# A hybrid decoder step: six first products ahead of 1/rms, the last two FFN groups by token halves, finished blocks parked tile by tile

## Chip, core and metric

The kernel runs on one core of a Trainium2 chip. The metric is the device time of one execution in microseconds; the median of three executions of the kernel before is 3283.72 us (3283.42 to 3285.11). A core has a matrix engine (TensorE, PE in the rows), a vector engine (VectorE, DVE), a scalar engine (ScalarE, ACT), GpSimd (POOL) and a queue that only issues transfers (SyncE, SP). Each engine takes its instructions in order; between engines there are semaphores. TensorE multiplies out of SBUF into PSUM banks, and the other engines read the banks. TensorE's clock is granted by a throttle; the windows show it as a share of full speed, and 0.50 and 1.00 are its two levels (1.2 and 2.4 GHz).

## What is computed

One layer for 2048 prompt tokens and 64 new tokens (8 sequences of 8), with a final norm. Shortened:

```python
h = rmsnorm(x, norm_attn); p = h @ w_in
o_attn = attention(q, k, v); o_rwkv = rwkv7_mixer(...)
gates = sigmoid(p[..., e4:] + b_gate)
merged = gates[..., :D] * (o_attn @ w_branch_attn) + gates[..., D:] * (o_rwkv @ w_branch_rwkv)
x = x + merged @ w_out
u = rmsnorm(x, norm_ffn) @ w_ffn_in; gp, vp = u[..., :D_FF], u[..., D_FF:]
c = cb + sum(cw[j] * buf[:, j:j + T] for j in range(3))      # buf: gp with two rows of state ahead
x = x + (gelu(c) * vp) @ w_ffn_out
y = rmsnorm(x, norm_final)                                    # x * rsqrt(mean(x*x) + 1e-6) * g
```

The outputs are y, the attention windows, and the shift, wkv and convolution states of both kinds of sequences. D is 1024, D_FF is 2816 (22 tiles of 128).

## The kernel before

The 2112 tokens go through the layer in three blocks b of T = 704 tokens. Activations lie with channels on the 128 partitions, so x of a block is 8 tiles of 128 x 704, and a block's tokens are worked on in two halves of 384 and 320 (`HALF`). A product is `mm3`: both operands are split into a high and a low part, and each step of 128 in depth takes three matmuls, 24 for a depth of 1024, 12 and 6 for the FFN's output products over 4 or 2 tiles of D_FF. A weight tile comes through `unit`: SP loads 512 KB into a raw buffer (L339, two of them), ScalarE casts the high part (L340), VectorE subtracts for the low part (L341), into one of two `wp` buffers. Products take PSUM banks of the pool `psd` (three), other work those of `psr` (three) and `psc` (two).

`start` begins the first block. It loads x by halves, scales and squares it, and multiplies the weight tiles js = (18, 19) with the unnormalised x, since 1/rms is a factor per token that can come later: three of four products go into the three `psd` banks, the fourth waits until one is free. 1/rms of a half is `rowsums` (L416 on TensorE), a chain of eleven small instructions on VectorE (`rms`, `rsqrt`, L423, L375 to L380), a transposition on TensorE (`turned`, L1039) and a copy to `rb0` on ScalarE (L488); `timed` (L508) is the multiplication that empties a bank. `proj` takes the products made ahead from `ahead`.

Each block then goes through projections, attention and the recurrent mixer, `branches` (L1346 to L1362: two half-depth products per half, gates on VectorE, the result into the tile `ms`, named `o` in the rows), `merge` and `ffn`. `ffn` takes the 22 tiles f in the groups GRP of 4, 4, 4, 4, 4 and 2: first products and activation for each f into the tile `ff` (L1432 to L1448), then the output products that are added to x (L1459 to L1461), 16 per group. In a group of 4 the halves alternate, in the last group of 2 the first half goes ahead of the second. After the last addition to a tile of x, `done` squares it (L394 on ScalarE, L395 on VectorE).

In blocks 0 and 1 the finished x is parked in DRAM: `final` issues one transfer per half on ScalarE's queue, after the half's last tile (L1477). The next block's `ms` tile of `branches` lies on the memory of that x, and so waits for the transfer. The final norm of a parked block is done later in a side stream (`final_steps`), which a planner puts between the products by a clock of estimated costs.

In block 2 `final_last` norms in place after all products: both halves' row sums, chains and transpositions, the copies to `rbl` (L1518), then for odd k a scale on ScalarE (L1521) and a product on GpSimd (L1522), for even k one instruction on VectorE (L1529), and eight transfers of tile pairs to the output yT on SP (L1530).

## Time and profile before

| | us |
|---|---|
| median of three executions | 3283.72 (3283.42 to 3285.11) |
| the profiled execution, its own time | 3283.15 |
| its span in the trace | 3281.2 |
| TensorE busy in it | 3242.3 |
| idle of TensorE ended by the first weight | 7.6 |
| idle ended by 1/rms and its use at the start | 4.7 and 2.5 |
| idle ended by `branches`' gate products, once | 3.8 |
| from TensorE's last big product to the end of the span | 18.3 |

TensorE is busy for 99% of the span, at a mean granted clock of 0.992. The last row runs from 3262.9 (the products that begin at 3247.22 last 15.64 us) to 3281.2. An engine's idle time is written at the instruction that ended it, with the instruction that released it.

### The profile page before, as it was taken

How to read it: one execution, taken by the hardware profiler on the slowest of the kernel's cores; microseconds unless marked ns; L12 is line 12 of the kernel's file. 1: busy time of each engine (PE TensorE's matmuls, PEld its weight loads, DVE VectorE, ACT ScalarE, POOL GpSimd, SP SyncE). 2: the span in 40 equal slices, each digit the busy share in tenths (PEclk: the TensorE clock that was granted, in tenths of full speed). 3: DMA queues.
4: the chain of work that ended last, by engine and by line, in shares of the span. 5: the costliest groups of instructions: out<-in, count | busy, mean ns of one | idle time of the engine just before them, and what ended most of it. 6: DMA issues, size and time to landing. Idle time of an engine off the chain costs nothing.

```text
span 3281.2 us, 60116 instructions
## 1 busy us (share of the span) xinstructions
PE 3242.3 (99%) x24072; PEld 3128.9 (95%) x24072; DVE 2029.4 (62%) x4596; ACT 1219.5 (37%) x2278; POOL 39.8 (1%) x104
## 2 busy tenths in 40 slices
PE   8999999999999999999999999999999999999998
PEld 7999999999999988899999999999999999999998
DVE  6676667745555576666555678755456575555555
ACT  4455433343323566623222323332223233222323
POOL 0000000000000000000000000000000000000000
PEclk9999999999999999999999999999999999999999
DMA  4644454545555633222433363253313272222222
GB/s 133 192 140 126 133 161 140 149 143 155 179 176 186 196 104 105 88 69 83 140 121 121 123 222 105 79 173 112 111 63 130 84 238 93 65 71 66 70 71 70
DMA packets 335016, 408.78 MB, mean 125 GB/s; under 512 B 110480, under 2 KB 261008, under 8 KB 334480
## 3 DMA queue, kind: packets, MB, share of 16 engines
q1 hardware_dynamic: 330576, 399.17, 39.0%
q10 hardware_dynamic: 4160, 5.77, 0.5%
q8 instruction: 189, 3.10, 0.4%
q14 instruction: 91, 0.75, 0.1%
HBM read 307.41 MB, written 98.41 MB: 124 GB/s over the span
## 4 chain that ended last, share of the span: by engine, by line
PE 96%; DVE 1%; ACT 1%; DMA 1%; issue 0%; POOL 0%; SPq 0%; POOLq 0%; DVEq 0%; ACTq 0%
PE psd L354 83%; PE psr L978 2%; PE psr L681 1%; PE psr L729 1%; PE psr L716 1%; PE psc L1148 1%; PE psc L1178 1%; PE psc L1181 1%; PE psr L868 1%; DMA xd<-x 0%; PE psc L1005 0%; PE psr L966 0%; PE psc L1183 0%; PE psc L1175 0%; PE psr L1005 0%; PE psc L1277 0%
## 5 line engine op out<-in xcount | busy, mean ns | idle before, releaser
L354 PE MATMUL psd<-o,wp 128*128 128x320 f32 (+1 forms) x8640 | 1443.7, 325 | 4.1 <-DVE m L1356 3.8
L354 PEld LDWEIGHTS psd<-o,wp 128*128 128x128 f32 x8640 | 1392.6, 188 | 16.3 <-issue 8.0
L354 PE MATMUL psd<-h,wp 128*128 128x320 f32 (+1 forms) x5184 | 911.7, 329 | 12.3 <-ACT wp L340 7.6
L354 PEld LDWEIGHTS psd<-h,wp 128*128 128x128 f32 x5184 | 838.1, 189 | 25.4 <-ACT wp L340 7.6
L340 ACT CAST wp<-wr 128x1024 fp32r<-128x1024 f32 x354 | 371.1, 1048 | 669.1 <-PE psd L354 643.3
L354 PE MATMUL psd<-ff,wp 128*128 128x384 f32 (+1 forms) x3168 | 536.1, 327 | 0.0
L341 DVE TENSOR_TENSOR wp<-wr,wp 128x1024 fp32r<-128x1024 f32 x354 | 432.8, 1222 | 164.9 <-ACT wp L340 157.8
L354 PEld LDWEIGHTS psd<-ff,wp 128*128 128x128 f32 x3168 | 515.3, 189 | 4.2 <-issue 1.0
L1461 DVE TENSOR_TENSOR x<-x,psd 128x384 f32<-128x384 f32 (+1 forms) x288 | 148.2, 519 | 200.7 <-PE psd L354 199.5
L1432 DVE TENSOR_TENSOR gb<-psd,rb 128x64 f32<-128x64 f32 (+2 forms) x154 | 70.5, 470 | 197.7 <-PE psd L354 195.2
L1433 ACT ACTIVATE cc<-gb,pt 128x64 f32<-128x64 f32 (+2 forms) x154 | 95.5, 636 | 209.4 <-DVE gb L1432 207.5
L1435 DVE SCALAR_TENSOR_TENSOR cc<-gb,pt,cc 128x704 f32<-128x704 f32 (+1 forms) x132 | 121.9, 924 | 2.2 <-ACT cc L1433 1.7
L1425 DVE TENSOR_TENSOR up<-psd,rb 128x384 f32<-128x384 f32 (+1 forms) x132 | 68.8, 521 | 64.4 <-PE psd L354 64.1
L1444 ACT ACTIVATE cc<-cc 128x704 f32<-128x704 f32 x66 | 52.4, 794 | 140.0 <-DVE cc L1435 82.9
L346 DVE TENSOR_TENSOR ff<-cc,ff 128x384 fp32r<-128x384 f32 (+1 forms) x132 | 68.5, 520 | 32.2 <-ACT ff L345 32.1
L1295 ACT ACTIVATE g<-psd,der 128x384 f32<-128x384 f32 (+1 forms) x64 | 35.5, 554 | 140.4 <-PE psd L354 89.2
L345 ACT CAST ff<-cc 128x384 fp32r<-128x384 f32 (+1 forms) x132 | 64.0, 486 | 61.6 <-DVE cc L1447 61.4
L624 ACT ACTIVATE s<-s,nm 128x256 f32<-128x256 f32 (+2 forms) x136 | 65.8, 486 | 39.0 <-DVE nm L619 36.8
L1447 DVE TENSOR_TENSOR cc<-cc,up 128x384 f32<-128x384 f32 (+1 forms) x132 | 68.9, 523 | 18.0 <-ACT cc L1444 14.5
L1356 DVE SCALAR_TENSOR_TENSOR m<-gt,psd 128x384 f32<-128x384 f32 (+1 forms) x96 | 49.6, 518 | 36.3 <-PE psd L354 35.5
L823 ACT ACTIVATE xs<-psd,der 128x384 f32<-128x384 f32 (+1 forms) x56 | 31.1, 555 | 107.4 <-PE psd L354 107.4
L395 DVE TENSOR_TENSOR acc<-acc,sq 128x384 f32<-128x384 f32 (+1 forms) x126 | 65.2, 518 | 6.2 <-ACT sq L394 5.5
(255 smaller groups left out, 2782.3 us busy)
## 6 DMA issues: line engine op xcount, KB each, us to landing
wr<-in_w_fi SPq DMA_DIRECT2D x132, 512.0 KB, 3.5
wr<-in_w_in SPq DMA_DIRECT2D x108, 512.0 KB, 3.7
wr<-in_w_fo SPq DMA_DIRECT2D x66, 512.0 KB, 3.5
cm<-md SPq DMA_DIRECT2D x33, 512.0 KB, 5.1
gt<-gd SPq DMA_DIRECT2D x48, 352.0 KB, 4.3
md<-m SPq DMA_DIRECT2D x48, 256.0 KB, 2.7
wr<-in_w_br SPq DMA_DIRECT2D x24, 512.0 KB, 4.3
wr<-in_w_out SPq DMA_DIRECT2D x24, 512.0 KB, 3.9
```

The costliest lines, as they stand in the source:

```text
L340: nc.scalar.copy(w[:, 0], raw)
L341: nc.vector.tensor_tensor(w[:, 1], raw, w[:, 0].bitcast(F32), op=ALU.subtract)
L346: self.nc.vector.tensor_tensor(lo, src, hi.bitcast(F32), op=ALU.subtract)
L354: nc.tensor.matmul(ps[:, :n], w[:, a, wk * 128:(wk + 1) * 128], act[:, k0 + k, b, c0:c0 + n], start=(start and k == 0 and j == 0), stop=(s ...
L624: nc.scalar.activation(s[:nq, h, :nk], s[:nq, h, :nk], ACT.Exp, bias=nm[:nq, h:h + 1], scale=0.125, accum_out=rs[:nq, h:h + 1])
L978: nc.tensor.matmul(pss[r_][:, c * 128:(c + 1) * 128], kb[rows, u + c], ar[rows, u + c], start=True, stop=True)
L1425: nc.vector.tensor_tensor(up[:, c0:c0 + n], ps[:, :n], rb[:, c0:c0 + n], op=ALU.mult)
L1432: nc.vector.tensor_tensor(dst, view(ps, 0), view(rb, c0), op=ALU.mult)
L1433: nc.scalar.activation(view(c, c0), dst, ACT.Identity, bias=self.par("cb", f), scale=cw[2])
L1435: nc.vector.scalar_tensor_tensor(c[:, :npr], gb[:, u:u + npr], cw[u], c[:, :npr], op0=ALU.mult, op1=ALU.add)
L1447: nc.vector.tensor_tensor(cv, cv, up[:, c0:c0 + n], op=ALU.mult)
L1461: nc.vector.tensor_tensor(xv, xv, ps[:, :n], op=ALU.add)
```

## The change

Three places change.

In `start` three weight tiles instead of two, (18, 19, 10), are multiplied ahead of 1/rms: six products in the three `psd` and the three `psr` banks, in the order first halves of 18 and 19, second halves of both, both halves of 10. `timed` is called for all six when `proj` takes them.

In `ffn` the loop's body is split into `first` and `second`, whose code is that of before. In the last block the groups from f = 16 (4 tiles) and from f = 20 (2 tiles) go together: the first products of all six f, then the output products of the first half for both groups, then those of the second half for both. The four weight tiles of the group from 16 are kept in `room`, on memory of the pool `old` that is free by then, the two of the other group in `wp`. The norm of the first half is a generator, stepped after six of the eight products of the group from 16 in the second half: row sums, transposition, and then VectorE's scalings with their transfers. After the last product only the second half is normed, with three of its eight tiles by ScalarE and GpSimd.

In `final` each tile of x is parked by its own transfer, 16 per block instead of two, right after the tile's square.

The diff, cut: the body of `first` is that of the loop before, indented otherwise.

```diff
@@ -460,7 +460,7 @@
-        js = (18, 19)
+        js = (18, 19, 10)
...
-        ps = [[self.dbank() for _ in js], [self.dbank()]]
+
+        banks = iter([self.bank(k) for k in "dddrrr"])
+        ps = {}
-        for u in range(2):
-            self.mm3(ps[0][u], w[u], self.h, *HALF[0])
-            if u == 0:
-                r = rms(0)
-        spread(r, 0)
-        self.mm3(ps[1][0], w[0], self.h, *HALF[1])
-        r = rms(1)
-        first = self.timed(ps[0][0], 0)
-        ps[1].append(self.dbank())
-        self.mm3(ps[1][1], w[1], self.h, *HALF[1])
-        spread(r, 1)
-        self.ahead = {js[0]: lambda: [first, self.timed(ps[1][0], 1)],
-                      js[1]: lambda: [self.timed(ps[hf][1], hf) for hf in range(2)]}
+        for u, hf in ((0, 0), (1, 0), (0, 1), (1, 1), (2, 0), (2, 1)):
+            if u == 2 and hf == 0:
+                w.append(self.unit(self.i["w_in"][js[2]]))
+            ps[u, hf] = next(banks)
+            self.mm3(ps[u, hf], w[u], self.h, *HALF[hf])
+            if u == 1:
+                r = rms(hf)
+                spread(r, hf)
+        self.ahead = {j: lambda u=u: [self.timed(ps[u, hf], hf) for hf in range(2)] for u, j in enumerate(js)}
...
-    def ffn(self, b, x, h2, rb, mp, done):
...
-        for f0, nf in GRP:
-            ft = mp.tile([P, 4, 2, T], F32R, tag="ff", name="ff")
-            for q in range(nf):
...
+        def first(f0, q, ft):
+
+            f = f0 + q
+            gb = mp.tile([P, 722], F32, tag="gb", name="gb")
...
+        def second(f0, nf, ft, order, ws, to=None, norm=None):
+
             per = 8 // nf
-            order = [(j, h) for j in range(8) for h in range(2)]
-            if per == 4:
-                order.sort(key=lambda u: u[1])
-            ws = {}
             for j, hf in order:
                 if j // per not in ws:
-                    ws[j // per] = self.unit(self.i["w_fo"][f0 + j // per])
+                    ws[j // per] = self.unit(self.i["w_fo"][f0 + j // per], None if to is None else to[:, j // per])
                 c0, n = HALF[hf]
                 ps = self.dbank()
                 self.mm3(ps, ws[j // per], ft, c0, n, nk=nf, wk0=(j % per) * nf)
@@ -1461,6 +1457,27 @@
                 nc.vector.tensor_tensor(xv, xv, ps[:, :n], op=ALU.add)
                 if f0 + nf == FF:
                     done(hf, j)
+                if norm and nf == 4 and j not in (1, 3):
+                    next(norm, None)
+
+        halves = [[(j, h) for j in range(8)] for h in range(2)]
+        for f0, nf in GRP[:-2] if last else GRP:
+            ft = mp.tile([P, 4, 2, T], F32R, tag="ff", name="ff")
+            for q in range(nf):
+                first(f0, q, ft)
+            second(f0, nf, ft, sum(halves, []) if nf == 2 else [(j, h) for j in range(8) for h in range(2)], {})
+        if last:
+
+            room = self.bigtile(dead, "o")[:].rearrange("p a b c -> p (a b c)")
+            fts = [mp.tile([P, 4, 2, T], F32R, tag="ff", name="ff"),
+                   room[:, 8192:8192 + 4 * T].rearrange("p (a b c) -> p a b c", a=2, b=2)]
+            for (f0, nf), ft in zip(GRP[-2:], fts):
+                for q in range(nf):
+                    first(f0, q, ft)
+            tos, ws = (room[:, :8192].rearrange("p (a b c) -> p a b c", a=4, b=2), None), ({}, {})
+            for order in halves:
+                for (f0, nf), ft, to, w in zip(GRP[-2:], fts, tos, ws):
+                    second(f0, nf, ft, order, w, to, norm if order[0][1] else None)
 
@@ -1473,10 +1490,9 @@
             self.square(accs[hf][:, :n], x[:, j, c0:c0 + n], j, n)
-            if j == KT - 1:
-                nc.scalar.dma_start(self.xd[b][:, :, c0:c0 + n], x[:, :, c0:c0 + n])
-                if hf:
-                    self.push("n", self.final_steps(b, accs))
+            nc.scalar.dma_start(self.xd[b][:, j, c0:c0 + n], x[:, j, c0:c0 + n])
+            if j == KT - 1 and hf:
+                self.push("n", self.final_steps(b, accs))
...
@@ -1510,33 +1526,35 @@
 
         def norm(hf):
             c0, n = HALF[hf]
-            yield 0.2
             r = self.rms(self.rowsums(accs[hf], n, "r"), "r")
-            yield 0.2
+            yield
             pb = self.turned(r, "r")
-            rb = fp.tile([P, 384], F32, tag=("cc", "up")[hf], name="rbl")
-            nc.scalar.copy(rb[:, :n], pb[:, :n])
-            for k in range(1, KT, 2):
-                xv = x[:, k, c0:c0 + n]
-                nc.scalar.activation(xv, xv, ACT.Copy, scale=self.par("norm_final", k))
-                nc.gpsimd.tensor_tensor(xv, xv, rb[:, :n], op=ALU.mult)
-                if hf == 0:
-                    yield
-            if hf == 0:
-                yield 60.0
+            if hf:
+                rb = fp.tile([P, 384], F32, tag="up", name="rbl")
+                nc.scalar.copy(rb[:, :n], pb[:, :n])
+            yield
             for k in range(0, KT, 2):
-                xv = x[:, k, c0:c0 + n]
-                nc.vector.scalar_tensor_tensor(xv, xv, self.par("norm_final", k), pb[:, :n], op0=ALU.mult, op1=ALU.mult)
+                for u in range(2):
+                    xv = x[:, k + u, c0:c0 + n]
+                    if u and hf and k < 6:
+                        nc.scalar.activation(xv, xv, ACT.Copy, scale=self.par("norm_final", k + u))
+                        nc.gpsimd.tensor_tensor(xv, xv, rb[:, :n], op=ALU.mult)
+                    else:
+                        nc.vector.scalar_tensor_tensor(xv, xv, self.par("norm_final", k + u), pb[:, :n],
+                                                       op0=ALU.mult, op1=ALU.mult)
                 nc.sync.dma_start(self.o["yT"][:, k:k + 2, b * T + c0:b * T + c0 + n], x[:, k:k + 2, c0:c0 + n])
+                yield
+        norms = [norm(0), norm(1)]
 
         def done(hf, j):
             c0, n = HALF[hf]
-            acc, xv = accs[hf][:, :n], x[:, j, c0:c0 + n]
-            self.square(acc, xv, j, n)
-            if j == KT - 1:
-                self.push("mn"[1 - hf], norm(hf))
-
-        return done
+            self.square(accs[hf][:, :n], x[:, j, c0:c0 + n], j, n)
+            if hf and j == KT - 1:
+                for _ in norms[1]:
+                    pass
+
+        return done, norms[0]
...
-    def ffn_stage(self, b, x, h2, rb):
+    def ffn_stage(self, b, x, h2, rb, dead=None):
...
-            self.ffn(b, x, h2, rb, fp, self.final_last(b, x, fp) if b == NB - 1 else self.final(b, x))
+            self.ffn(b, x, h2, rb, fp, *(self.final_last(b, x, fp) if b == NB - 1 else (self.final(b, x), None)), dead)
             if b == NB - 1:
-                self.drain("m", "n")
...
-        self.ffn_stage(2, *xs)
+        self.ffn_stage(2, *xs, old)
```

TensorE at the start, before (`psd<-h,wp` are big products, `psc<-ct,acc` row sums, `psc<-ct,nwyd` the transposition of 1/rms):

```order
L354 MATMUL psd<-h,wp 128x320 x15
L416 MATMUL psc<-ct,acc 128x1 x3
L354 MATMUL psd<-h,wp 128x320 x8
L1039 MATMUL psc<-ct,nwyd 128x128 x3
L416 MATMUL psc<-ct,acc 128x1 x3
L354 MATMUL psd<-h,wp 128x320 x24
L1039 MATMUL psc<-ct,nwyd 128x128 x3
L354 MATMUL psd<-h,wp 128x384 x24
L354 MATMUL psd<-h,wp 128x320 x24
```

and after:

```order
L354 MATMUL psd<-h,wp 128x320 x8
L354 MATMUL psr<-h,wp 128x320 x22
L354 MATMUL psr<-h,wp 128x384 x2
L354 MATMUL psr<-h,wp 128x320 x2
L354 MATMUL psr<-h,wp 128x384 x22
L354 MATMUL psr<-h,wp 128x320 x4
L1037 MATMUL psc<-ct,nwyd 128x128 x3
L416 MATMUL psc<-ct,acc 128x1 x3
L354 MATMUL psr<-h,wp 128x320 x18
L354 MATMUL psd<-h,wp 128x384 x24
L1037 MATMUL psc<-ct,nwyd 128x128 x3
L354 MATMUL psd<-h,wp 128x320 x24
```

The transposition of the first half's 1/rms stood behind 72 matmuls and stands behind 126 now; that of the second half stands behind all six products and one product of the next projection.

ScalarE at the passage from block 0 to block 1, before (`sq` and `acc` are squares, `wp<-wr` casts of weights, `xd<-x` the parking, `o<-m` the first result of `branches`):

```order
L391 ACTIVATE acc<-x_12416 128x320
L394 ACTIVATE sq<-x_12416 128x320 x2
L340 CAST wp<-wr 128x1024
L394 ACTIVATE sq<-x_12416 128x320 x3
L340 CAST wp<-wr 128x1024
L394 ACTIVATE sq<-x_12416 128x320
L1477 DMA xd_276<-x_12416 1024x1x320
L394 ACTIVATE sq<-x_12416 128x320
L340 CAST wp<-wr 128x1024
L1361 ACTIVATE o<-m 128x384
```

and after:

```order
L1493 DMA xd_276<-x_12416 128x320
L394 ACTIVATE sq<-x_12416 128x320
L1493 DMA xd_276<-x_12416 128x320
L340 CAST wp<-wr 128x1024
L394 ACTIVATE sq<-x_12416 128x320
L1493 DMA xd_276<-x_12416 128x320 x2
L394 ACTIVATE sq<-x_12416 128x320
L1493 DMA xd_276<-x_12416 128x320
L394 ACTIVATE sq<-x_12416 128x320
L1359 ACTIVATE o<-m 128x384
L340 CAST wp<-wr 128x1024
L1359 ACTIVATE o<-m 128x320
```

Parking transfers now stand between the squares; the first `o<-m`, which waits for all of them, follows the last square directly, ahead of a weight's cast that stood ahead of it.

VectorE at the end of block 2, before (`x<-x,psd` adds a product to x, `x<-x,pt,psr` scales a tile by 1/rms):

```order
L379 TENSOR_TENSOR nwtd<-nwtd,rmsm 128x3 x2
L380 SCALAR_TENSOR_TENSOR nwyd<-nwtd,nwyd 128x3 x2
L378 SCALAR_TENSOR_TENSOR nwtd<-nwyd 128x3
L379 TENSOR_TENSOR nwtd<-nwtd,rmsm 128x3
L380 SCALAR_TENSOR_TENSOR nwyd<-nwtd,nwyd 128x3
L1529 SCALAR_TENSOR_TENSOR x_28569<-x_28569,pt,psr 128x320 x4
L1529 SCALAR_TENSOR_TENSOR x_28569<-x_28569,pt,psr 128x384 x4
```

and after, in the second half's products:

```order
L1457 TENSOR_TENSOR x_28597<-x_28597,psd 128x320
L378 SCALAR_TENSOR_TENSOR nwtd<-nwyd 128x3
L379 TENSOR_TENSOR nwtd<-nwtd,rmsm 128x3
L380 SCALAR_TENSOR_TENSOR nwyd<-nwtd,nwyd 128x3
L1457 TENSOR_TENSOR x_28597<-x_28597,psd 128x320 x2
L1543 SCALAR_TENSOR_TENSOR x_28597<-x_28597,pt,psr 128x384 x8
L1457 TENSOR_TENSOR x_28597<-x_28597,psd 128x320 x5
L395 TENSOR_TENSOR acc<-acc,sq 128x320
L1457 TENSOR_TENSOR x_28597<-x_28597,psd 128x320
L395 TENSOR_TENSOR acc<-acc,sq 128x320
```

Eight scalings of the first half now stand between the sixth and the seventh addition of the second half's first eight.

## Rows read from the trace of the kernel before

**Rows 1.** TensorE's timeline at the start: start us, duration us, instructions [idle before <- releaser].
```profile
22.61 1.42 PE L354 MATMUL psd<-h,wp 128*128 128x320 f32 x8
28.73 0.90 PE L1039 MATMUL psc<-ct,nwyd 128*128 128x128 f32 x3 [4.70 <-DVE nwyd L380]
...
36.09 0.49 PE L1039 MATMUL psc<-ct,nwyd 128*128 128x128 f32 x3
39.04 24.98 PE L354 MATMUL psd<-h,wp 128*128 128x384 f32 x153 [2.47 <-DVE p L508]
```

**Rows 2.** VectorE's timeline at the start: a chain of 1/rms, products multiplied by it.
```profile
30.74 0.16 DVE L423 TENSOR_SCALAR rmsm<-psc 128x3 f32<-128x3 f32 x1
...
33.44 0.16 DVE L380 SCALAR_TENSOR_TENSOR nwyd<-nwtd,nwyd 128x3 f32<-128x3 f32 x1
...
38.51 0.95 DVE L508 TENSOR_TENSOR p<-psd,rb 128x320 f32<-128x320 f32 x2
```

**Rows 3.** ScalarE's timeline at the start, the copy of a turned 1/rms.
```profile
37.24 0.42 ACT L488 COPY rb<-psc 128x320 f32<-128x320 f32 x1
```

**Rows 4.** One-microsecond windows at the start; the granted clock stands ahead of the DMA share.
```profile
28.00:29.00 1.00, 0.28 (x2) 0.28 (x3) 0.56 (x4) 0.00 (x0) 0.00 (x0) 0.50 0.76 279
34.00:35.00 1.00, 1.00 (x7) 1.00 (x6) 0.00 (x0) 0.00 (x0) 0.00 (x0) 0.73 0.00 0
37.00:38.00 1.00, 0.00 (x0) 0.00 (x0) 0.64 (x1) 0.66 (x2) 0.00 (x0) 1.00 0.00 0
```

**Rows 5.** TensorE's timeline from block 0 to block 1.
```profile
1897.26 15.55 PE L354 MATMUL psd<-o,wp 128*128 128x384 f32 x96
1916.58 18.70 PE L354 MATMUL psd<-o,wp 128*128 128x384 f32 x99 [3.77 <-DVE m L1356]
```

**Rows 6.** The chain that ended last, there: start us, duration us, what.
```profile
1897.98 16.37 DMA xd<-x
```

**Rows 7.** DMA issues between 1885 and 1925: count, KB each, median us to landing.
```profile
wr<-in_w_br SPq DMA_DIRECT2D x4, 512.0 KB, 5.6
xd<-x ACTq DMA_DIRECT2D x1, 1536.0 KB, 6.0
...
xd<-x ACTq DMA_DIRECT2D x1, 1280.0 KB, 16.4
```

**Rows 8.** Windows of the same place, columns as in group 4.
```profile
1902.00:1914.00 12.00, 10.81 (x70) 10.55 (x68) 3.89 (x7) 1.05 (x1) 0.00 (x0) 1.00 1.05 403
1919.00:1920.00 1.00, 1.00 (x5) 1.00 (x4) 1.00 (x2) 0.47 (x1) 0.00 (x0) 0.50 0.37 93
1922.00:1923.00 1.00, 1.00 (x7) 1.00 (x6) 0.00 (x0) 0.00 (x0) 0.00 (x0) 0.95 0.77 254
```

**Rows 9.** ScalarE's timeline there: a square, the issue of a transfer.
```profile
1896.67 0.47 ACT L394 ACTIVATE sq<-x 128x320 f32<-128x320 f32 x1 [1.46 <-DVE x L1461]
...
1897.98 0.52 ACTq L1477 DMA_DIRECT2D xd<-x  x1
```

**Rows 10.** TensorE's timeline over the last 160 us.
```profile
3123.59 61.94 PE L354 MATMUL psd<-o,wp 128*128 128x384 f32 x384
...
3264.48 1.50 PE L416 MATMUL psr<-ct,acc 128*128 128x1 f32 x12 [1.61 <-DVE acc L395]
```

**Rows 11.** Groups from 3255 to the end: count | busy us, mean ns | idle.
```profile
L1461 DVE TENSOR_TENSOR x<-x,psd 128x320 f32<-128x320 f32 x8 | 3.9, 484 | 0.0
```

**Rows 12.** Timeline of the last 20 us: the scalings on VectorE and GpSimd.
```profile
3269.28 4.02 DVE L1529 SCALAR_TENSOR_TENSOR x<-x,pt,psr 128x320 f32<-128x320 f32 x8 [0.94 <-ACT rbl L1518]
3269.33 7.11 POOL L1522 TENSOR_TENSOR x<-x,rbl 128x320 f32<-128x320 f32 x8 [508.05 <-ACT rbl L1518]
```

**Rows 13.** DMA issues of the last 16 us.
```profile
out_yT<-x SPq DMA_DIRECT2D x4, 320.0 KB, 2.5
```

**Rows 14.** One window while the last outputs leave, columns as in group 4.
```profile
3272.00:3279.00 7.00, 0.00 (x0) 0.00 (x0) 1.31 (x3) 0.00 (x0) 4.44 (x5) 0.50 1.04 361
```

More of the change, by code (lines that the diff above doesn't have):

```diff
@@ L1396, in merge, with ffn @@
         return x, h2, rb
-    def ffn(self, b, x, h2, rb, mp, done):
+    def ffn(self, b, x, h2, rb, mp, done, norm, dead):
         nc = self.nc
@@ L1463, in ffn @@
                     done(hf, j)
+                if norm and nf == 4 and j not in (1, 3):
[6 more added lines that the diff above has]
+            second(f0, nf, ft, sum(halves, []) if nf == 2 else [(j, h) for j in range(8) for h in range(2)], {})
+        if last:
+            room = self.bigtile(dead, "o")[:].rearrange("p a b c -> p (a b c)")
[8 more added lines that the diff above has]
+                    second(f0, nf, ft, order, w, to, norm if order[0][1] else None)
     def final(self, b, x):
@@ L1512, in norm @@
             c0, n = HALF[hf]
[L1513 removed]
             r = self.rms(self.rowsums(accs[hf], n, "r"), "r")
[L1515 removed]
+            yield
             pb = self.turned(r, "r")
[L1517 to L1529 removed]
+            if hf:
+                rb = fp.tile([P, 384], F32, tag="up", name="rbl")
+                nc.scalar.copy(rb[:, :n], pb[:, :n])
+            yield
+            for k in range(0, KT, 2):
+                for u in range(2):
[3 more added lines that the diff above has]
+                        nc.gpsimd.tensor_tensor(xv, xv, rb[:, :n], op=ALU.mult)
+                    else:
+                        nc.vector.scalar_tensor_tensor(xv, xv, self.par("norm_final", k + u), pb[:, :n],
+                                                       op0=ALU.mult, op1=ALU.mult)
                 nc.sync.dma_start(self.o["yT"][:, k:k + 2, b * T + c0:b * T + c0 + n], x[:, k:k + 2, c0:c0 + n])
+                yield
+        norms = [norm(0), norm(1)]
         def done(hf, j):
             c0, n = HALF[hf]
[L1534 to L1539 removed]
+            self.square(accs[hf][:, :n], x[:, j, c0:c0 + n], j, n)
[3 more added lines that the diff above has]
+        return done, norms[0]
     def rwkv_prep(self, b, ep, sts, between):
```

80 lines of the change are left out of this document (38 added, 42 removed).

## Prediction

> **What bounds the kernel now.** The busy times on the page come first: TensorE works in 3242.3 of 3281.2 us at a mean granted clock of 0.992, so nothing can be won where it runs through; what counts is the 39 us in which it stands and the stretches at half clock. Next comes its list of waits, and then its timeline at each of them. At the start it stands for 4.70 us until the first 1/rms is there and for 2.47 us until a bank is emptied [rows 1]. Around the first stop the windows show the granted clock at 0.50, its lower level, and 0.73 in the window from 34 us, back at 1.00 after that; in the second, shorter stop it stays at 1.00 [rows 4]. At the passage from block 0 to block 1 it stands for 3.77 us [rows 5]; the chain of waits puts 16.37 us of parking transfer ahead of that [rows 6], and the clock is at 0.50 until shortly after 1922 [rows 8]. At the end the last row sums begin at 3264.48 [rows 10], and 16.7 us go by until the span ends at 3281.2, with no big product left.
>
> **The start.** Removed are both stops, 4.70 + 2.47 = 7.17, and the half clock. The 0.73 says that 0.54 of its window was at half clock, so from the restart at 28.73 to 34.54 TensorE ran at half speed, which cost 5.81 / 2 = 2.9. Together 10.1.
> What is late next: at 22.61 + 1.42 = 24.03 [rows 1] 72 of the 144 matmuls of the six products are done, 48 of 384 columns and 24 of 320. At full clock 384 matmuls, half of each size, take 61.94 us [rows 10]; split by columns that is 0.176 for one of 384 and 0.146 for one of 320. The 24 + 48 that are left take 4.2 + 7.0 = 11.2, row sums and one transposition in between 0.9 (a transposition is 0.49 [rows 1]), so the six are done at 36.2. The next product has a bank, since the first half's 1/rms is long there, and ends at 40.4; then the second half's transposition, 40.9. The product behind it needs a bank of `psd` that only the second half's 1/rms empties: the copy takes 0.42 [rows 3], two multiplications 0.95 [rows 2], so 42.3 and a stop of 1.4. The chain itself (30.74 to 33.60, 2.9 us [rows 2]) is no limit: its row sums stand 18 matmuls ahead of the end of the six, at some 33.5. The stop is shorter than the 2.47 at which the clock stayed up, so I add no half clock. Bounds: 0, if VectorE takes the two in the better order, and 3.8, if a weight's subtraction and two more instructions come first, with another 1.5 of half clock. Net -8.7, from -10.1 to -5.
>
> **Parking by tiles.** Removed at the first passage: the stop, 3.77, and half clock from 1916.58 to 1922.1 (0.95 in the window from 1922 leaves 0.1 of it), 5.5 / 2 = 2.75; together 6.5. At the second passage TensorE's waits show no stop, so nothing is to be had there. Before, 1280 KB were asked for at 1897.98 and were there at 1914.35, in traffic of 403 GB/s with the DMA engines' share at 1.05 [rows 6 to 8]; that is 78 GB/s for this transfer. Now all but four or five tiles of 160 KB are on their way before the next block's loads begin. At 78 GB/s a tile takes 2.05 us; from about 1896.5 that is 8 to 10 us for the last ones, 1905 to 1907. Needed is the memory at about 1908: TensorE then has work until 1897.26 + 15.55 = 1912.8 [rows 5], and the way from the release to its restart was 1914.35 to 1916.58, 2.2 us. So the stop goes, with little to spare. Behind the waiting first result of `branches` on ScalarE stands the cast of the third weight; it is due with the third pair of products, at the same 1912.8, and behind it a subtraction, so a late landing would show there as well.
> Added are 14 issues per block at 0.52 on ScalarE, beside a square of 0.47 [rows 9]: 1.0 per tile against 0.88 that TensorE takes for the six matmuls of a tile. ScalarE falls back by 8 x 0.12 = 1 us plus the casts of two weights, which reach TensorE a little late: I take 0.4 at each of two passages (0 to 2 each). Net -5.7, from -6.5 to -2.5 if the memory comes in time.
> Against it speaks a rule of the Trainium skill, "DMA: Bandwidth & Descriptors", section "Rules for kernel authors": many small transfers should be coalesced into one large one, and full bandwidth wants 1 MiB and more per transfer. By that rule the 16 tiles would get through later than the two halves, which is the first rival below. The trace is on neither side alone: 320 KB landed in 2.5 us on emptier queues [rows 13], 1536 KB in 6.0 [rows 7], so five small ones would take longer than one large one only if nothing overlapped.
>
> **The end.** After the last row sums begin, 16.7 us remain before. The chain, the turn and a copy to the first scaling take 3269.3 - 3264.48 = 4.8, with two halves' small instructions interleaved; one half alone I put at 4.4. From the first scaling to the end are 11.9, in which eight products on GpSimd take 7.11 and eight scalings on VectorE 4.02 [rows 12], and 2.88 MB leave. Now three on GpSimd (2.7) and five on VectorE (2.5) are left, and 1.31 MB. At the 361 GB/s of before [rows 14] 2.88 MB take 8.0 and 1.31 MB 3.6, and the 3.9 us of lead and landing that were left stay: 7.5, and as GpSimd's third product gates a pair I take 8. Tail 4.4 + 8 = 12.4, -4.3.
> Against that: the first half's row sums and transposition are in TensorE's stream, 0.4 + 0.5 = 0.9. VectorE has eight scalings in a row (8 x 0.53 = 4.2, from 4.02 for four of each size [rows 12]) ahead of the seventh addition. They start when the transposition is done, 76 matmuls into the second half: 76 x 0.146 + 0.35 = 11.5 us. They and one addition of 0.48 [rows 11] end at 16.2. The seventh and eighth product and one of the next group fill the three banks by 8 x 1.76 + 0.88 = 14.9; with the 0.2 of an engine's handover TensorE stands for 1.1 to 1.5. I take 1.1, as the copies and squares of the tail are no later for it. The weights of `room` come through the two raw buffers twice as often per us in the first half (one for two products instead of four): two of the four can be prepared during the first products, the others take a load each within the 4.2 us of two products; I put 0.5 (0 to 3). Net -4.3 + 0.9 + 1.1 + 0.5 = -1.8, from -4.3 to +2.
>
> **Sum.** -8.7 - 5.7 - 1.8 = -16.2. The profiled execution took 3283.15, the median is 3283.72, 0.57 above: 3266.95 on the first, 3267.5 on the second. What is moved in the rest of the program is small: the big products are the same number, and the small ones stand at nearly the same places between them.
>
> **The rivals.**
> Parked too late: the tiles do not get through before 1908 and stop and half clock return at the first passage. For it: saturated engines and 78 GB/s for this queue. Against it: most of the data leaves earlier. 3267.5 + 6.5 = 3274. Chance 0.15; it is also what the rule above would bring.
> The end gains nothing: VectorE's queue and the weights' buffers cost 3 to 5 more. For it: VectorE has both halves' adds and scalings, and squares come after. Against it: 8 x (0.48 + 0.48) is less than the 8 x 1.76 of the first group's products. 3267.5 + 4 = 3271.5. Chance 0.17.
> The start keeps half: the second 1/rms comes 2 us later and the clock falls as it did after the 4.70. For it: VectorE also has the weight's subtraction and the work of the next projections. Against it: the stop was shorter by far than 4.70. 3267.5 + 5 = 3272.5. Chance 0.12.
> Slower: the transfers wait for one another on ScalarE's queue. If a transfer can only be issued when the fourth before it has landed, and each takes the 5.9 us of the large ones or the 5.6 of a weight in this traffic [rows 7], 16 tiles take 16 x 5.9 / 4 = 24 us against 15.4 of TensorE; the casts behind them are 8.6 late, with 2.7 of half clock 11.3 per block, 22.6 for two. With the start and the end that is 3283.72 - 8.7 - 1.8 + 22.6 = 3296. It decides from a landing of 15.4 / 4 = 3.9 us per tile on; 320 KB took 2.5. Chance 0.05.
> The change doesn't do what it says: moving work by the planner's costs opens a stop elsewhere that takes the gain back, or two of the first three come together: 3278 to 3284. Chance 0.08.
>
> **Chances and range.** The forecast has 0.43; its own range is 3262 to 3271. A difference of 0.2%, 6.6 us, is about what a measurement can tell here. Forecast and the first three rivals lie below 3277: faster 0.87. Within 6.6 us of 3283.72 lies the last rival: 0.08. Slower 0.05. The range for 8 in 10 goes from 3261 (the end costs nothing against it, the start and the passages by their good ends) to 3276 (first rival with some loss at the start).
>
> **What would show it.** In the profile after: no idle above 2.5 us on TensorE before 45 us and a granted clock of 1.00 from 20 to 45; the first result of `branches` in block 1 not released by a parking transfer after 1908, and no half clock there; parking transfers that land in 2 to 4 us; the eight scalings in the last half in one row on VectorE, with a stop of about 1 us behind them; some 12.4 us from the last row sums to the end. Wrong it would be by a stop above 3 us at any of these three places, or by a new one in the weights of the first half.

## The result, and the profile after

The changed kernel takes 3266.89 us in the median of six executions (3264.84 to 3267.88), the kernel before 3283.57 beside it (3280.67 to 3285.11): a ratio of 0.995, 95% interval 0.9937 to 0.9963, 16.7 us less. In two later sets, of five executions each, it took 3266.57 against 3280.96 and 3267.55 against 3282.37, 14.4 and 14.8 us less. The forecast was 3267.5; the kernel before itself moved between 3280.88 and 3283.57 from set to set. The profiled execution took 3264.84, its span is 3263.1.

TensorE's waits in the changed kernel (what waits, for whom: us in total, times, longest) show what is left:

```profile
PE psd L354 <- ACT wp L340: 8.1, 1, 8.1
PE psr L1037 <- DVE nwyd L380: 4.8, 2, 2.5
...
PE psr L416 <- DVE acc L395: 1.6, 1, 1.6
PE psd L354 <- DVE p L506: 1.1, 1, 1.1
PE psd L354 <- ACT ff L345: 1.0, 1, 1.0
PE psd L354 <- DVE x L1457: 1.0, 1, 1.0
PE psd L354 <- DVE ff L346: 0.5, 1, 0.5
PE psd L354 <- DVE up L1422: 0.4, 1, 0.4
```

The stops of 4.70 and 2.47 us at the start and of 3.77 at the first passage [rows 1, 5] are gone. New are 1.1 behind L506 (the multiplication by 1/rms), 1.0 behind L1457 (the addition to x at the end) and three short ones, 2.0 us together, behind `ff` and `up`, the last activations of an FFN.

The start, TensorE's timeline, to be held against [rows 1], and the windows against [rows 4] (the granted clock ahead of the DMA share):

```profile
22.29 1.42 PE L354 MATMUL psd<-h,wp 128*128 128x320 f32 x8
...
35.47 4.32 PE L354 MATMUL psd<-h,wp 128*128 128x384 f32 x24
...
41.22 7.98 PE L354 MATMUL psd<-h,wp 128*128 128x320 f32 x48 [1.10 <-DVE p L506]
```

```profile
28.00:29.00 1.00, 1.00 (x8) 1.00 (x7) 0.16 (x1) 0.00 (x0) 0.00 (x0) 1.00 0.94 377
40.00:41.00 1.00, 0.12 (x2) 0.00 (x0) 0.33 (x1) 0.42 (x1) 0.00 (x0) 1.00 0.87 356
```

The clock stays at 1.00, its upper level, also in the window with most of the stop of 1.10.

The passage from block 0 to block 1, TensorE's and ScalarE's timelines, against [rows 5, 9]:

```profile
1869.42 0.79 PE L354 MATMUL psd<-ff,wp 128*128 128x384 f32 x3 [0.40 <-DVE up L1422]
1871.25 0.79 PE L354 MATMUL psd<-ff,wp 128*128 128x384 f32 x3 [1.04 <-ACT ff L345]
1872.56 11.63 PE L354 MATMUL psd<-ff,wp 128*128 128x384 f32 x60 [0.53 <-DVE ff L346]
...
1888.34 36.87 PE L354 MATMUL psd<-o,wp 128*128 128x384 f32 x227
```

```profile
1889.56 0.47 ACTq L1493 DMA_DIRECT2D xd<-x  x1
...
1895.62 0.53 ACT L1359 ACTIVATE o<-m 128x384 fp32r<-128x384 f32 x1 [4.00 <-DMA xd<-x]
```

TensorE now goes through from 1888.34 without a stop. The first result of `branches` still waits for a parking transfer, but only until 1895.62, 7.3 us after the first product of `branches`; before, the transfer landed 17.1 us after it (1914.35 against 1897.26). The new stops lie ahead of that, at 1869 to 1872.5, and the clock goes to half behind them:

```profile
1873.00:1876.00 3.00, 3.00 (x11) 3.00 (x10) 2.17 (x4) 1.57 (x3) 0.28 (x1) 0.50 0.91 290
```

The end, TensorE's and VectorE's timelines, against [rows 10, 12]:

```profile
3230.70 0.72 PE L416 MATMUL psr<-ct,acc 128*128 128x1 f32 x6
...
3242.94 6.43 PE L354 MATMUL psd<-o,wp 128*128 128x320 f32 x42 [0.97 <-DVE x L1457]
3250.97 0.83 PE L416 MATMUL psr<-ct,acc 128*128 128x1 f32 x6 [1.61 <-DVE acc L395]
```

```profile
3238.20 4.29 DVE L1543 SCALAR_TENSOR_TENSOR x<-x,pt,psr 128x384 f32<-128x384 f32 x8 [0.43 <-PE psr L1037]
3242.41 1.27 DVE L1457 TENSOR_TENSOR x<-x,psd 128x320 f32<-128x320 f32 x3
...
3255.69 2.38 DVE L1543 SCALAR_TENSOR_TENSOR x<-x,pt,psr 128x320 f32<-128x320 f32 x5 [1.52 <-ACT rbl L1534]
```

From the last row sums to the end of the span it is 3263.1 - 3250.97 = 12.1 us, 16.7 before.

Since both kernels issue the same 16992 big matmuls (line L354) and, apart from the start and the last 600, in the same order, the start of the n-th can be compared between traces. The table gives that start less the one of the kernel before, in us; "end" is the difference of the spans.

| kernel | first | 480 | 4080 | 8000 | 9000 | 9120 | 9360 | 15840 | end |
|---|---|---|---|---|---|---|---|---|---|
| changed | +0.5 | -10.1 | -10.1 | -10.2 | -13.3 | -8.9 | -15.4 | -15.4 | -18.1 |
| changed, second profile | +0.1 | -9.6 | -9.6 | -8.2 | -11.2 | -6.8 | -13.2 | -13.2 | -15.7 |
| changed, third profile | +1.0 | -8.8 | -8.8 | -7.4 | -10.5 | -5.7 | -12.1 | -12.1 | -14.9 |
| start alone | 0.0 | -10.3 | -10.4 | -10.2 | -11.8 | -9.4 | -9.4 | -9.4 | -9.6 |
| parking alone | +0.3 | -1.0 | -1.0 | -1.1 | -4.1 | -4.2 | -10.7 | -10.7 | -11.0 |
| end alone | +0.8 | +0.8 | +0.8 | +1.0 | -2.0 | -2.0 | -2.6 | -2.6 | -5.4 |
| start and end | -0.1 | -9.7 | -9.7 | -8.4 | -11.4 | -7.0 | -9.9 | -9.9 | -12.5 |

Up to 480 it is the start, from 9120 to 9360 the passage, from 15840 on the end. Between 4080 and 9120 nothing was changed in the program, and yet the columns differ. Parking alone and end alone have TensorE's order of the kernel before up to there and run 3 us faster than the one profile of before, all of it between 8000 and 9000: clock stretches come and go between executions. A place that shows it (windows of the kernel before, then of parking alone, the same stretch of the program):

```profile
1714.00:1720.00 6.00, 6.00 (x23) 6.00 (x23) 3.81 (x14) 1.04 (x1) 0.44 (x2) 0.50 0.00 0
```

```profile
1713.00:1719.00 6.00, 6.00 (x40) 6.00 (x40) 5.19 (x18) 1.05 (x1) 0.44 (x2) 1.00 0.14 52
```

Held against those two, and not against the one profile of before, the kernels with the new start run 4 to 6 us slower in this stretch (-9.4 + 10.4 = +1.0 for start alone, +2.7 for start and end, +1.2, +2.8 and +3.1 for the three profiles of the changed kernel, against -3.2 and -2.8). Most of it is lost from 9000 to 9120, where the stops near 1870 lie: 4.4 to 4.8 us in the changed kernel and in start and end, 2.4 in start alone, where the clock stays up behind them, nothing in the other two. The other place is near 1400, where TensorE never stops but is longer at half clock (windows of the kernel before, then of the changed kernel, whose other two profiles also have 9 us at 0.50 there):

```profile
1407.00:1413.00 6.00, 6.00 (x28) 5.36 (x28) 0.42 (x1) 0.00 (x0) 0.95 (x1) 0.50 0.03 5
```

```profile
1399.00:1408.00 9.00, 9.00 (x43) 8.21 (x43) 0.42 (x1) 0.00 (x0) 0.95 (x1) 0.50 0.05 9
```

It is worth 1.4 in the second and the third profile (from 4080 to 8000); the first has the same loss there but lacks another stretch of half clock, near 895. Why it is longer with the new start is open.

### The profile page after: what moved, and what is told of

The parts are those of the page before. It is cut to its first block, busy times and chain, and to the rows that moved or that the text cites. A ratio compares the mean times of both kernels' runs of the same rounds, so it can differ in the third digit from the quotient of the medians.

```text
span 3263.1 us, 60157 instructions
## 1 busy us (share of the span) xinstructions
PE 3234.3 (99%) x24072; PEld 3120.2 (96%) x24072; DVE 2033.1 (62%) x4601; ACT 1215.9 (37%) x2272; POOL 35.1 (1%) x99
## 4 chain that ended last, share of the span: by engine, by line
PE 82%; issue 16%; DVE 1%; DMA 0%; ACT 0%; POOL 0%; SPq 0%; POOLq 0%; ACTq 0%; DVEq 0%
PE psd L354 69%; PE psr L976 2%; PE psr L679 1%; PE psr L727 1%; PE psr L714 1%; PE psc L1146 1%; PE psc L1176 1%; PE psc L1179 1%; PE psr L866 1%; PE psc L1003 0%; PE psr L964 0%; PE psc L1181 0%; PE psc L1173 0%; PE psr L1003 0%; PE psc L1275 0%
## 5 line engine op out<-in xcount | busy, mean ns | idle before, releaser
L354 PE MATMUL psd<-o,wp 128*128 128x320 f32 (+1 forms) x8736 | 1458.8, 325 | 1.3 <-DVE x L1457 1.0
L354 PEld LDWEIGHTS psd<-o,wp 128*128 128x128 f32 x8736 | 1406.2, 188 | 13.7 <-issue 4.2
L354 PE MATMUL psd<-h,wp 128*128 128x320 f32 (+1 forms) x5112 | 895.7, 328 | 11.3 <-ACT wp L340 8.1
L354 PEld LDWEIGHTS psd<-h,wp 128*128 128x128 f32 x5112 | 823.0, 188 | 24.0 <-ACT wp L340 8.1
L341 DVE TENSOR_TENSOR wp<-wr,wp 128x1024 fp32r<-128x1024 f32 x350 | 427.9, 1222 | 161.2 <-ACT wp L340 154.6
L354 PE MATMUL psd<-ff,wp 128*128 128x320 f32 (+1 forms) x2880 | 488.7, 327 | 2.0 <-ACT ff L345 1.0
L354 PEld LDWEIGHTS psd<-ff,wp 128*128 128x128 f32 x2880 | 467.1, 189 | 7.5 <-issue 1.6
L1457 DVE TENSOR_TENSOR x<-x,psd 128x384 f32<-128x384 f32 (+1 forms) x288 | 148.0, 518 | 202.4 <-PE psd L354 201.6
L1430 ACT ACTIVATE cc<-gb,pt 128x64 f32<-128x64 f32 (+2 forms) x154 | 95.6, 636 | 198.1 <-DVE gb L1429 196.7
L345 ACT CAST ff<-cc 128x384 fp32r<-128x384 f32 (+1 forms) x128 | 62.0, 487 | 61.7 <-DVE cc L1444 61.4
```

The costliest lines, as they stand in the source:

```text
L341: nc.vector.tensor_tensor(w[:, 1], raw, w[:, 0].bitcast(F32), op=ALU.subtract)
L354: nc.tensor.matmul(ps[:, :n], w[:, a, wk * 128:(wk + 1) * 128], act[:, k0 + k, b, c0:c0 + n], start=(start and k == 0 and j == 0), stop=(s ...
L1430: nc.scalar.activation(view(c, c0), dst, ACT.Identity, bias=self.par("cb", f), scale=cw[2])
L1457: nc.vector.tensor_tensor(xv, xv, ps[:, :n], op=ALU.add)
```

## Experiments

**Each part alone.** Three kernels have one of the three edits of the diff each, one has the start and the end and parks as before.

> Only the six first products at the start; parking and the end as before. Theory (three independent parts, and the new start makes the planner deal the side streams of all blocks anew): about 10 us are won before 45 us; the stop of 3.8 us and the half clock at the passage from block 0 to block 1 are still there; and the stops on TensorE that the changed kernel shows near 1869 us, ended by the last activations of block 0's FFN (2.0 us in all), are there too. Total -8 to -10 against before, 3274 to 3275.5. Rival (the stops near 1869 come from the parking transfers on ScalarE's queue): none of them here, and the total is -10 to -12.

> Only the parking by tiles; TensorE's order is that of before. Theory: the stop of 3.8 us and the half clock at the first passage go, nothing else changes, -6.5: 3277. Rival (parking delays ScalarE and with it the activations of the FFN's last group): new stops of some 2 us and half clock ahead of the passage, -2 to -3: 3281.

> Only the last two FFN groups by token halves. Theory: the tail behind the last row sums falls from 16.7 to 12.1 us, TensorE gets 0.9 of row sums and transposition and a stop of 1.0 behind the eight scalings, nothing from the weights kept: -2.7, 3281. Rival (the weights or VectorE's queue cost 3 us and more): 0 or above, 3283.5 to 3286.

> The changed kernel with the parking of before (two transfers per block). Theory: what the parking gives is its own, so the stop at the passage and its half clock are back and the time is 6.5 above the changed kernel's 3266.9: 3273.4. Rival (the stops near 1869 have moved TensorE so that the passage would have been free anyway): no stop at the passage, within 2 us of 3266.9.

Measured, medians beside 3282.04 of the kernel before: start 3273.35 (ratio 0.9975, 0.9967 to 0.9984), parking 3273.81 (0.9978, 0.9969 to 0.9987), end 3279.98 (0.9994, 0.9985 to 1.0003), start and end 3271.69 (0.9968, 0.9956 to 0.998). So -8.7, -8.2, -2.1 and -10.4. The interval of the end alone includes 1, so its gain rests on the profiles; parking came out 1.7 us better than expected, which its interval (4 to 10 us) allows.

The start alone has the stops at the FFN's end and that at the passage (TensorE's timeline):

```profile
1872.23 0.80 PE L354 MATMUL psd<-ff,wp 128*128 128x384 f32 x3 [1.04 <-ACT ff L345]
1873.54 10.29 PE L354 MATMUL psd<-ff,wp 128*128 128x384 f32 x60 [0.52 <-DVE ff L346]
...
1907.33 7.87 PE L354 MATMUL psd<-o,wp 128*128 128x384 f32 x31 [3.87 <-DVE m L1354]
```

Parking alone has neither; TensorE works straight through the passage, and ScalarE's wait ends 7.1 us after its first product:

```profile
1890.36 2.88 PE L354 MATMUL psd<-ff,wp 128*128 128x320 f32 x18
1893.08 32.22 PE L354 MATMUL psd<-o,wp 128*128 128x384 f32 x199
```

```profile
1900.15 0.53 ACT L1361 ACTIVATE o<-m 128x384 fp32r<-128x384 f32 x1 [4.85 <-DMA xd<-x]
```

That settles two things. The stop at the passage belongs to the parking, in the table -6.4 to -6.5 in every kernel that parks by tiles. And the stops at 1869 to 1872 belong to the start, not to the parking's load on ScalarE, which was the rival. How an edit at 30 us can reach 1870 shows in the programs: with the new start the scheduler orders the small work of blocks 0 and 1 differently. Before, all sixteen casts of block 1's gathered branch inputs (`o<-ol`) stand on ScalarE ahead of the activations of block 0's last tile of D_FF; now six of them stand between these, and an activation waits in the queue behind a cast that waits for its load (ScalarE's timeline of the changed kernel; L345 is the cast, L1430 the activation):

```profile
1861.92 0.87 ACT L345 CAST o<-ol 128x384 fp32r<-128x384 f32 x2 [1.87 <-DMA ol<-rd]
...
1864.42 0.65 ACT L1430 ACTIVATE cc<-gb,pt 128x320 f32<-128x320 f32 x1
```

Start and end without the parking has the passage's stop again, shorter: 1.82 us in its profile, against 3.77, 3.87 and 2.8 in the other three kernels with two transfers per block. The stop follows the time the large transfer took to land: 16.4 us in the kernel before and in start alone (3.77 and 3.87), 15.5 in end alone (2.8), 14.4 in start and end (1.82). So the rival, that TensorE would be late enough to pass freely, is not borne out: start alone has the stops near 1870 too, and the full stop at the passage. +4.8 us against the changed kernel were measured and 6.5 expected. End alone gives from matmul 15840 to the end -2.8 in its profile; the theory said -2.7.

**The sum.**

> The changed kernel, unaltered, beside the three that follow. Against before by the three parts measured alone (start 8.7, parking 8.2, end 2.1 us below before, start and end together 10.4): if they added up -19; theory (the start's new dealing costs a stop ahead of the passage, and the passage is worth less behind it) -16 to -17; 3265 to 3267. The stops on TensorE near 1869 us, 2.0 in all, come again, since the order is the same.

Measured 3266.57 beside 3280.96: -14.4, less than the -16 to -17 expected; in the other two sets it was -16.7 and -14.8. The parts add up to -19, 2 to 5 us more. Start and end add up (-8.7 and -2.1 alone, -10.4 together); what is missing lies with the parking, 8.2 alone and 4.8 beside the other two (3271.69 against 3266.89). The profiles show part of it: at the passage the table gives start and end -2.9 without the new parking, by the faster landing above, so that the tiles add only 3.5 there of the 6.5 they are worth against the kernel before. The stops near 1870 are no part of it, since start alone and start and end pay for them already. One profile does not tell whether the large transfer always lands faster in start and end, and the rest, some 2 us, is within the scatter of the sets.

**Why parking by tiles is in time.** Two readings were possible: the data leaves earlier, or small transfers get a larger share of the DMA engines. In a first kernel for this the tiles were to be issued after the half's last one:

```diff
-            nc.scalar.dma_start(self.xd[b][:, j, c0:c0 + n], x[:, j, c0:c0 + n])
+            if j == KT - 1:
+                for k in range(KT):
+                    nc.scalar.dma_start(self.xd[b][:, k, c0:c0 + n], x[:, k, c0:c0 + n])
```

> The changed kernel, but the eight tiles of a half are parked after the half's last tile, by eight transfers in a row, so the transfers are small and late. Theory (what helps is that most of the data leaves before the next block's loads): the first result of the branches waits again until 8 to 14 us after the last tile, TensorE stops for 1 to 4 us there and gets half clock: +3 to +6 against the changed kernel. Rival (many small transfers get a larger share of the engines than one large one, whenever they are issued): no stop, within 1 us of the changed kernel.

It took 3267.2, but the scheduler had moved the transfers back between the squares, so it was the changed kernel once more and decides nothing. In the second the eight transfers are held behind the half's last square (`self.squared` is that instruction), and a third parks four tiles a transfer:

```diff
-            nc.scalar.dma_start(self.xd[b][:, j, c0:c0 + n], x[:, j, c0:c0 + n])
+            if j == KT - 1:
+                with self.tc.issue_after(self.squared):
+                    for k in range(KT):
+                        nc.scalar.dma_start(self.xd[b][:, k, c0:c0 + n], x[:, k, c0:c0 + n])
```

```diff
-            nc.scalar.dma_start(self.xd[b][:, j, c0:c0 + n], x[:, j, c0:c0 + n])
+            if j % 4 == 3:
+                nc.scalar.dma_start(self.xd[b][:, j - 3:j + 1, c0:c0 + n], x[:, j - 3:j + 1, c0:c0 + n])
```

> The changed kernel, but the eight tiles of a half are parked by eight transfers that stand behind the half's last square on ScalarE's queue; in the run late_tiles the scheduler had put them back between the squares, so that one was the changed kernel again and told nothing. Theory (what helps is that most of the data leaves before the next block's loads): the passage waits as with two transfers, a stop of 1 to 3 us and half clock, +3 to +5 against the changed kernel's 3266.6. Rival (many small transfers get a larger share than one large one, whenever they are issued): no stop, within 1 us of it.

> The changed kernel, but x is parked by four tiles a transfer, two transfers per half. Theory (early data): the last 640 KB at the 78 GB/s seen before take 8 us, land some 3 us ahead of need, no stop: within 1 us of the changed kernel. Rival (small transfers are what helps): the last transfer is as slow as the whole half was, a stop of 1 to 2 us and half clock, +2 to +4.

Small and late: 3273.96 beside 3280.88, 7.4 us above the changed kernel's 3266.57 of another set and more than the 3 to 5 expected. Four tiles a transfer: 3265.63 in the same set, 8.3 below small and late. With four tiles a transfer TensorE goes through the passage as with one:

```profile
1888.15 41.04 PE L354 MATMUL psd<-o,wp 128*128 128x384 f32 x253
```

The last of them, 640 KB, was issued at 1888.96, 0.8 us after the first product of `branches`, and landed 7.8 us later: 82 KB per us, where the single large transfers got 78 to 89 (1280 KB in 16.4 to 14.4 us). So leaving early is enough, without a larger share of the engines. TensorE's and ScalarE's timelines of the small and late one:

```profile
1892.35 1.31 PE L354 MATMUL psd<-o,wp 128*128 128x384 f32 x6
1894.62 13.02 PE L354 MATMUL psd<-o,wp 128*128 128x384 f32 x78 [0.97 <-DVE wp L341]
1908.40 2.03 PE L354 MATMUL psd<-o,wp 128*128 128x320 f32 x12 [0.76 <-DVE m L1354]
1911.18 24.09 PE L354 MATMUL psd<-o,wp 128*128 128x384 f32 x148 [0.75 <-DVE m L1354]
```

```profile
1897.69 7.84 ACTq L1496 DMA_DIRECT2D xd<-x  x8
1905.58 1.05 ACT L340 CAST wp<-wr 128x1024 fp32r<-128x1024 f32 x1 [7.42 <-DMA xd<-x]
1909.05 0.89 ACT L1359 ACTIVATE o<-m 128x384 fp32r<-128x384 f32 x2 [2.42 <-DMA xd<-x]
```

This run does not settle the rival, since its transfers leave later than meant: the eight issues begin 5.3 us after the first product of `branches` (1892.35), the large transfer of start and end 0.8 after it (1891.07 against 1890.26). From the first issue to the last landing (1905.21 and 3.7 more) the eight took 11.2 us, the large one 14.4 to 16.4. Begun at 0.8 they would by these numbers have landed 12.0 after the first product, an estimate; in the kernel before TensorE had work for 15.55 from there, and 2.2 went by between landing and restart, so 13.3 would have done. Whether small transfers alone, issued late, would be enough stays open.

Eight issues in a row take 7.84 us, 0.33 each would make 2.6, and the cast of a weight behind them comes after 7.42 us of idle. Six are issued by 1900.9, before any of the eight has landed. The seventh waits until 1901.98, the eighth until 1905.21. The chain of waits shows for what the seventh did:

```profile
1895.73 6.22 DMA wr<-in_w_br
1901.95 0.02 issue
1901.98 5.50 DMA xd<-x
```

It is a weight's load of SP's queue, whose semaphore the seventh transfer uses next; for the eighth it is a load of the next block's x, issued at 1896.12 and landed 9.1 us later. So transfers do wait on ScalarE's queue, with the cast behind them, as the prediction's slower rival has it, but here for an earlier load of SP's queue and not for the fourth parking transfer before them.

**The stops at the FFN's end.** The subtractions of the gathered inputs were put on GpSimd, for block 1:

```diff
-                self.split(os_[:, k, 0, c0:c0 + n], os_[:, k, 1, c0:c0 + n], t[:, c0:c0 + n])
+                hi, lo = os_[:, k, 0, c0:c0 + n], os_[:, k, 1, c0:c0 + n]
+                self.nc.scalar.copy(hi, t[:, c0:c0 + n])
+                low = self.nc.gpsimd if pool else self.nc.vector
+                low.tensor_tensor(lo, t[:, c0:c0 + n], hi.bitcast(F32), op=ALU.subtract)
```

> The changed kernel, but the low parts of block 1's gathered branch inputs are subtracted on GpSimd instead of VectorE (16 instructions of 0.5 us less on VectorE between 1853 and 1869). Theory (the stops near 1869 come from these subtractions, which the new dealing has put between the last activations of block 0's FFN): the stops go, with the half clock behind them, -2 to -3.7 against the changed kernel. Rival (ScalarE's casts or late loads make the stops): they stay, within 0.5.

Measured 3267.96, 1.4 above the changed kernel beside it, which is within the scatter of the two (3265.7 to 3269.69 against 3264.32 to 3267.83). The stops stay, 1.32 and 1.39 us. VectorE got free of 16 instructions, but its others became slower while GpSimd worked (VectorE's timeline; the same instructions take 1.22 for L341 and 1.9 for two of the convolution's without it):

```profile
1866.88 2.06 DVE L341 TENSOR_TENSOR wp<-wr,wp 128x1024 fp32r<-128x1024 f32 x1 [2.62 <-ACT wp L340]
1868.86 3.18 DVE L1435 SCALAR_TENSOR_TENSOR cc<-gb,pt,cc 128x704 f32<-128x704 f32 x2
```

And ScalarE's queue was as before: one activation stood behind casts that waited 1.70 us for their load (ScalarE's timeline; L1314 is the cast, L1433 the activation):

```profile
1865.03 0.87 ACT L1314 CAST o<-ol 128x384 fp32r<-128x384 f32 x2 [1.70 <-DMA ol<-rd]
1865.81 1.04 ACT L340 CAST wp<-wr 128x1024 fp32r<-128x1024 f32 x1
1866.75 0.65 ACT L1433 ACTIVATE cc<-gb,pt 128x320 f32<-128x320 f32 x1
```

So the theory is not borne out, but the run does not refute it either: the edit took 16 instructions off VectorE and made those that were left slower. That the late loads on ScalarE's queue are the cause is what the rows suggest, also VectorE's own wait of 2.62 for the cast behind them; a kernel that takes the loads forward was not tried, so it stays open.

**The end.** Three of the first half's scalings go to ScalarE and GpSimd; then the same with four tiles a transfer, beside the changed kernel:

```diff
-            if hf:
-                rb = fp.tile([P, 384], F32, tag="up", name="rbl")
-                nc.scalar.copy(rb[:, :n], pb[:, :n])
+            rb = fp.tile([P, 384], F32, tag=("cc", "up")[hf], name="rbl")
+            nc.scalar.copy(rb[:, :n], pb[:, :n])
...
-                    if u and hf and k < 6:
+                    if u and k < 6:
```

> The changed kernel, but three of the eight scalings of the first half go to ScalarE and GpSimd, as those of the second half do. Theory (TensorE's stop of 1.0 us ten products into the second half is the eight scalings ahead of VectorE's next addition): five take 2.7 us, the addition comes in time, the stop goes, -1.0. Rival (the sum of VectorE's work up to the end decides): the gain is swallowed at the last addition, 0.

> The two small gains together: parking by four tiles a transfer, and three of the first half's eight scalings on ScalarE and GpSimd. Theory: the stop of 1.0 us in the second half is gone and the passage is as free as with 16 transfers, so -1 to -2 against the changed kernel beside it. Rival (both differences, 0.9 and 0.7 us, were scatter between executions): within 0.5 of it.

> The changed kernel, unaltered, for the comparison with the run beside it: 3265 to 3267.

Measured 3265.85 beside 3266.57 for the first, 3266.08 beside 3267.55 for both together; this third set of the changed kernel is 0.55 above the range expected of it. The stop of 0.97 is gone; five scalings take 2.71 us instead of eight in 4.29 (TensorE and VectorE of the first):

```profile
3240.33 3.18 PE L354 MATMUL psd<-ff,o 128*128 128x320 f32 x20
3243.35 7.37 PE L354 MATMUL psd<-o,wp 128*128 128x320 f32 x48
```

```profile
3241.13 2.71 DVE L1542 SCALAR_TENSOR_TENSOR x<-x,pt,psr 128x384 f32<-128x384 f32 x5 [0.94 <-ACT rbl L1533]
```

-0.7 and -1.5 have the sign expected, and both kernels have the lowest medians of their sets; the ratios to the kernel before, 0.9951 (0.9939 to 0.9964) and 0.9949 (0.9935 to 0.9962), overlap with the changed kernel's, 0.9954 and 0.9955, so the times do not show a gain of this size. The profiles do, for the stretch alone: from matmul 15840 to the end of the span the two kernels gain 4.2 and 3.7 us on the kernel before, the three profiles of the changed kernel 2.5 to 2.8. So the first theory holds, and its rival, that the last addition swallows the gain, does not.

## Why the prediction was right, and where it was not

**Start: -8.7 predicted, -8.8 to -10.3 measured.** The stop of 4.70 and the half clock went as said, and the stop of 2.47 shrank as said. The six products were done at 35.5 instead of 36.2, the stop that is left was 1.10 instead of 1.4, and the clock stayed up in it. What I had missed lies ahead of 24 us: the first matmul came 0.5 later than before (8.09 against 7.59; it varies by 1 us between the profiles), and by 22.29 TensorE had done 66 matmuls, two more than before by 22.61, since while x is loaded there is more to multiply.

**Parking: -6.5 for the stop and its clock predicted, -6.5, -6.4 and -6.4 measured.** The prediction allowed 10.7 us after the first product of `branches` for the landing (1908 against 1897.26) and put it at 7.7 to 9.7 (1905 to 1907); it came after 7.3. The single transfers landed after 1.8 to 5.9 us, 4.1 in the median, longer than the 2 to 4 named as a sign: they overlap. The cost of the issues, 0.4 at each passage, was not seen: an issue takes 0.33 in the median instead of 0.52, and it does not hold back the next square. The size of an early transfer made no difference between one tile and four (3266.57 and 3265.63, in two sets). Issued late and in a bunch the small ones came out 2.3 us above two large ones (3273.96 against 3271.69), also in two sets, whose intervals overlap. On transfer size the Trainium skill's "DMA: Bandwidth & Descriptors", "Rules for kernel authors", speaks for the large one. Its row on many small transfers names 64 KB, under which overhead prevails; these have 160 to 192, so no run here tests that figure.

**End: -1.8 predicted, -2.8, -2.5 and -2.8 measured.** Tail -4.6 instead of -4.3, by two errors in opposite directions: 4.7 us from the last row sums to the first scaling (3250.97 to 3255.69) instead of 4.4, and 7.4 from there to the end instead of 8. TensorE's extra work 0.8 instead of 0.9, the stop 0.97 instead of 1.1. The 0.2 for a handover between engines in the upper bound of that stop is more than the 0.14 at the passage of the kernel before, from the end of VectorE's last gate product (1916.44) to TensorE's restart (1916.58). Nothing is left for the weights' buffers, for which I had put 0.5: their four tiles were ready when they were needed.

**The rest of the program: nothing predicted, +4 to +6 measured.** This step failed: "What is moved in the rest of the program is small." The counts of big and small products were the same, and I looked at TensorE's order alone, where the small products stand at nearly the same places. What had moved is the order of casts and activations on ScalarE and VectorE, and of loads on SP's queue. The runs showed in its place the stops near 1870 with what follows, 2.4 to 4.8 us, and a longer stretch of half clock near 1400, worth 1.4. It was named among the rivals ("moving work by the planner's costs opens a stop elsewhere") but priced with 0.08, and in part it came true. Which of the moved instructions makes the stops stays open.

**The total** came out within 0.6 us in the first set; in the other two the gain was 14.4 and 14.8 instead of 16.2. The mechanisms of the three parts were right, and they gave 2 to 3 us more than forecast; the rest of the program took 4 to 6; and the profile of before, against which everything was summed, lost about 3 us more to half clock between 8000 and 9000 than two others with the same order of TensorE. That these nearly cancel is luck.

## What to carry to other kernels

A transfer that others wait for should start when its first data is ready: leaving early was enough here, and one tile or four per transfer made no difference. A bunch of issues waited here for loads of another queue, and held up the work behind it on its own queue. Products that wait unscaled in idle banks took a latency off the path here, and the clock stayed up through the stop that was left. Where a scheduler orders the engines, compare the order of every engine over the whole program, not of the bottleneck alone: an edit at 30 us opened a stop at 1870.

## What the runs showed of the hardware

Instructions of VectorE with two operands in SBUF slowed down while GpSimd worked on SBUF: 1.86 us in the mean instead of 1.22 for L341, 1.57 instead of 0.94 for the convolution's, 1.18 instead of 0.56 for the product `cc<-cc,up` of 384 columns. Those with an operand in PSUM did not (0.54 and 0.55 for 384 columns), nor did the final scalings (0.54 each of 384 columns, with and without GpSimd beside them). The Trainium skill's "SBUF — State Buffer", section "SBUF: two separate sides", says that the two share one pair of ports, which the one that starts first, a VectorE instruction with two SBUF inputs or a GpSimd instruction that reads SBUF, holds for its whole length while the other waits; the rows agree in which instructions slowed down.

A queue's issue of a transfer took 0.33 us in the median for a tile of 128 x 320 or 384 and 0.52 for a half of x in one; six in a row took 3.2. A transfer of 1280 KB landed after 14.4 to 16.4 us beside the loads of SP's queue, one of 1536 KB, issued 7.6 us earlier, after 6.0.

And stretches at half clock differ between executions. Parking alone and the kernel before have the same order of TensorE up to 1714, where the kernel before has 6 us at 0.50, which cost 3, and parking alone has 1.00. The changed kernel itself has 3 us at 0.50 from 895 in its second profile and 1.00 there in its first. A single profile of a kernel this long is good to about 3 us.
